# Two wide maxima of a unit move between the value products, and the turns get two buffers

## The chip, the cores and the metric

The kernel runs on one core of a Trainium2 chip. The core has TensorE (PE, with its weight loads listed apart as PEld), VectorE (DVE), ScalarE (ACT), GpSimd (POOL) and SyncE (SP), which here issues the DMAs. The metric is the device time of one launch, in microseconds (us). Before the change the median of three runs is 1690.89 us, from 1688.29 to 1691.36.

## The reference

Two layers of a diffusion backbone, each with an adaptive norm, a projection, attention, a SiLU gate and an output projection. Layer 0, which the change touches, is grouped-query attention: 16 heads share 4 key/value heads, a head has 64 columns. The 1024 latent tokens read 256 context keys and 1024 latent keys; the 256 context tokens read the context alone. All is in float32.

```python
def gqa_attend(q, k, v):
    s = jnp.einsum('bqhgd,bkhd->bhgqk', q, k).astype(jnp.float32) * (GQA_HEAD_DIM ** -0.5)
    p = jax.nn.softmax(s, axis=-1).astype(v.dtype)
    return jnp.einsum('bhgqk,bkhd->bqhgd', p, v)

def gqa_mixer(h, hc, p, cos, sin, with_ctx_out):
    ...
    k_all = jnp.concatenate([kc, k], axis=1)
    v_all = jnp.concatenate([vc, v], axis=1)
    o = sweep_query_blocks(lambda qb: gqa_attend(qb, k_all, v_all), q).reshape(B, S, GQA_WIDTH)
    y = (o * jax.nn.silu(g)) @ p["w_out"]
    ...
        oc = gqa_attend(qc, kc, vc).reshape(B, L, GQA_WIDTH)
```

## The kernel before

Layer 0's attention is worked off in 20 *units*: 16 *latent* units, one for each head (1024 queries, ten key tiles of 128, in `kts`), and four *context* units, one for each key/value head (its four heads' 256 queries, two key tiles). In order they are four latent, one context, four latent, one context, eight latent, two context. `Attention.run` takes them one after the other, with the order of PE, DVE and ACT as the code writes it; POOL and SP are ordered by a scheduler.

A latent unit has three stretches on PE:

- **Scores.** For each key tile a score tile `st` (128 keys by 1024 queries) is made of four pairs of products (L545): three for the split of queries and keys into a high and a low part, and one that subtracts each query's maximum, held in a row of `shift`. A pair is two products for the two halves of the queries, on rows 0 to 63 and 64 to 127 of the array, so 64 rows by 128 columns each. ACT makes the exponential `p` (L552). There are two buffers for `st`; the unit's value sum `avt` takes the place of one of them.
- **Turn and totals.** The maxima of a later unit, one for each query, stand in `m` with the queries on the partitions. `turn` (in `do_shift`) transposes them on PE into `mx` (L459), copies them on DVE to the row buffer `crow` (L461), and SP sends them from there to `shift` (L464). `crow` has one buffer. Then the totals of the softmax of an earlier unit are summed on PE, in `mx` (L645), and DVE transposes and inverts them there (L649, L650). `mx` has two buffers.
- **Value products.** `do_av` adds up 20 products with the values, two for each key tile (L600), each half in 64 columns of the array, so 128 rows by 64 columns. The trace has two records for each such product.

The maxima are made ahead. `next_maxima` hands out the steps of the units to come: a latent unit has ten *wide maxima*, eight over its latent keys (L421: two products of 512 columns into one `mx`, reduced by DVE in L430) and two over the context keys (L426, L432). One stands in front of each score tile of a latent unit (`count += 1` in `run`, then `scores_by_halves`). So during a latent unit the last six maxima of the next one and the first four of the one behind it are made, as a rule. The last latent unit (`last_lat`) has none left to make, and it is cut in two groups, of six and four tiles.

DVE also adds up the last four exponentials of a unit in pairs (L572, `pair_sum`), and POOL adds these sums and the first six exponentials (L586).

`run_turns` is called once for each group, between the scores and the value products, and runs all turns that are pending. Where a context unit's maxima have been finished together with those of a latent unit, it runs two, and three ahead of the last latent unit.

The same class makes layer 1's attention, with `WIDE` false: there the maxima are not wide, and `crow` comes from the common pool.

Of the kernel before, what the change touches and what calls it, by code (L numbers as in the profile page):

```python
# [11 lines left out]
F32R = mybir.dt.float32r  # L12
# [7 lines left out]
P = 128  # L20
# [9 lines left out]
WIDE = (True, False)  # L30


def raw(ap):
    return ap.bitcast(F32)
# [3 lines left out]
def hybrid_kernel(ctx: ExitStack, tc: tile.TileContext, ins: dict, out: bass.AP):  # L38
# [197 lines left out]
    class Plan:  # L236
# [8 lines left out]
        def run(self):  # L245
            engines = mybir.EngineType
            with tc.manual_schedule(engines={engines.PE, engines.Activation, engines.DVE, engines.Pool, engines.SP}):
                for _, _, fn, args in sorted(self.todo, key=lambda e: e[:2]):
                    fn(*args)
# [60 lines left out]
    class Attention:  # L310
# [134 lines left out]
        def do_shift(self, u):  # L445

            s = self.state[id(u)]
            if u["kind"] == "lat":
                m = self.sm.tile([P, 8], F32, name="m1", tag="m1")
                dve.reduce_max(m, s["m"], axis=AX.X)  # L450
            else:
                m = s["m"][:, :, 0]

            def turn():
                if not WIDE[self.l]:
                    t = self.ps_m.tile([P, 512], F32, name="mx", tag="mx")[:8, :P]
                else:
                    t = self.ps_m.tile([P, 1024], F32, name="mx", tag="mx")[:8, :P]
                pe.transpose(t, m, ident)  # L459
                r = self.sm.tile([8, P], F32R, name="crow", tag="crow", bufs=1)  # L460
                dve.tensor_copy(r, t)  # L461
                if HALVES[self.l]:
                    for n in range(2):
                        sp.dma_start(raw(s["crow"][n]), raw(r[4 * n:4 * n + 4, :]))  # L464
                else:
                    sp.dma_start(raw(s["crow"]), raw(r))

            self.turns.append(turn)

        def start_unit(self):  # L470
            u = self.units[self.started]
# [115 lines left out]
                s["sum"] = t  # L587
            s["total"] = ([s["sum"]] if held else []) + last

        def do_av(self, u, group, ps):  # L590

            s = self.state[id(u)]
            kts = u["kts"]
            if group[0] == kts[0]:
                if not WIDE[self.l]:
                    s["av"] = self.ps_o.tile([P, 512], F32, name="av", tag="av")
                s["v"] = self.load_v(u)
            for kt, p in zip(group, ps):
                for n in range(2):
                    pe.matmul(s["av"][64 * n:64 * n + 64, :], lhsT=s["v"][:, kt, u["vc"]:u["vc"] + 64],  # L600
                              rhs=p[:, n * 512:(n + 1) * 512], start=kt == kts[0], stop=kt == kts[-1])
            if group[-1] == kts[-1]:
                self.finish(u)
# [66 lines left out]

            self.totals.append(total)

        def run_turns(self):
            while self.turns:
                self.turns.pop(0)()

        def run(self, lead, ahead, extra, tail):

            count = lead
            parts = None  # L680
            with tc.manual_schedule(engines={mybir.EngineType.PE, mybir.EngineType.DVE, mybir.EngineType.Activation}):
                for t, u in enumerate(self.units):
                    kts = u["kts"]
                    for v in self.units[t:t + 2]:
                        self.load_v(v)
                    while self.started < min(t + 1 + ahead, len(self.units)):
                        self.start_unit()
                    whole = len(kts) > 4
                    cut = 6 if u is self.last_lat else 0

                    def one_more():
                        nonlocal count
                        count += 1
                        self.maxima(count, t + 1 + ahead)

                    for group in (kts[:cut], kts[cut:]):
                        if not group:
                            continue
                        end = group[-1] == kts[-1]
                        final = t == len(self.units) - 1 and end  # L700
                        p2s = [self.pp.tile([P, 2, 1024], F32, name="p", tag="p", bufs=5) for _ in range(len(group) // 2)]
                        ps = [p2[:, a, :] for p2 in p2s for a in range(2)]

                        late = not whole and t >= len(self.units) - 2
                        n1 = len(ps) - (4 if whole and end else 2 if late else 0)
                        for i, kt in enumerate(group):
                            self.run_deferred(self.step)
                            if HALVES[self.l]:
                                count += 1 if WIDE[self.l] else 2
                                self.scores_by_halves(u, kt, ps[i], self.next_maxima(count, t + 1 + ahead))  # L710
                            else:
                                self.do_scores(u, kt, ps[i], one_more)
                            self.step += 1
                            if i < n1:
                                self.add_up(u, [ps[i]], [])
                        if end and t + 2 < self.started:
                            self.state[id(self.units[t + 2])].pop("rest", lambda: None)()
                        if final:
                            tail()
                        if WIDE[self.l] and group[0] == kts[0]:  # L720
                            self.av_tile(u)
                        self.run_turns()
                        if late or final:
                            self.add_up(u, [], ps[n1:])
                        elif n1 < len(ps):
                            sums = [self.pair_sum(p2) for p2 in p2s[n1 // 2:]]
                            self.add_up(u, *(([], sums) if cut else (sums, [])))
                        if final:
                            self.run_deferred(self.step + 2)
                        gap = 0  # L730
                        while self.totals and (whole or late or final):
                            self.totals.pop(0)(gap)
                            gap += 3
                        if t % 2 and end:
                            if parts:
                                parts()
                            parts = extra.pop(0)() if extra else None
                        self.do_av(u, group, ps)
                        self.step += (2 + len(group)) // 3
                gap = 0  # L740
                while self.totals:
                    self.totals.pop(0)(gap)
                    gap += 3
            self.run_deferred(self.step)
# [373 lines left out]
    parts = [[ModPart(0, sec, q, 256, lambda: mp[0], 4, wk, ps_mod, ps_tp) for q in range(4)] for sec in range(2)]  # L1118
# [145 lines left out]
    def l0_open(at, st):  # L1264
        pool_ = st.enter_context(tc.tile_pool(name="shift0", bufs=1, **right))
        at.minus = pool_.tile([P, 4, P], F32R, name="minus")
        at.shift = pool_.tile([P, 512], F32R, name="shift")
        pool.memset(raw(at.shift), 0.0)
        for i in range(4):
            a, b = (ident[:, j:j + 1].broadcast_to([P, P]) for j in (i, 64 + i))  # L1270
            dve.scalar_tensor_tensor(at.minus[:, i, :], a, -1.0, b, op0=ALU.mult, op1=ALU.subtract)
# [89 lines left out]
    for g, pos in ((0, 4), (1, 9), (3, 18), (2, 19)):  # L1361
        units.insert(pos, ctxu[g])

    at = Attention(0, units, dict(scale=0.125, load=l0_load, scores=l0_scores, maxima=l0_maxima, mparts=1, open=l0_open, gaps=(4, 8, 11), kbufs=2, qbufs=3, vw=256))
    stE = ExitStack()
    with tc.tile_pool(name="wkg0a", bufs=4, **right) as wkg:
# [286 lines left out]
    for p_ in range(8):  # L1653
        for par in range(2):
            h = 2 * p_ + par
            units.append(dict(kind="lat", h=h, pair=p_, par=par, vg=(h // 4, 128 * (h // 2 % 2)), vc=64 * par,
                              kts=list(range(TT))))
    at = Attention(1, units, dict(scale=float(96 ** -0.5), load=l1_load, scores=l1_scores, maxima=l1_maxima, mparts=2, open=l1_open, gaps=(4, 6, 9),
                                  kbufs=3, qbufs=3, vw=128))
# [201 lines left out]
```

## Time and profile before

| | us |
|---|---|
| median of three runs | 1690.89 |
| the profiled execution, its own time | 1690.33 |
| its span, from the first to the last instruction | 1688.5 |
| first turn to last total of layer 0's attention | 376.7 to 741.9 |

The span is the part of the profiled execution that the trace shows; the 1.8 us around it belong to its own time too. A line of the page's groups reads: source line, engine, operation, output and inputs by the program's names, shape, count, then busy time and mean duration (ns) of one, then the idle time of the engine ahead of them and who ended it. The timeline lists instructions by their start and merges equal neighbours: with "x2", the two products of a pair. The idle time ahead and its releaser stand in brackets. PEclk, in the views by stretch, is the share of TensorE's full clock that was granted: three numbers from the end of a row, ahead of the DMA share and the GB/s.

```profile
L421 PE MATMUL mx<-KA,QA x256: 383/391/503, 317.2 to 685.0; 64*128 64x512 f32 x128
L600 PE MATMUL avt<-p,v x672: 592/592/1115, 376.9 to 740.4; 128*64 128x512 f32 x168
L461 DVE CAST crow<-mx x36: 267/278/280, 344.2 to 1562.5; 8x128 fp32r<-8x128 f32 x36
```

These three rows are of the views of single lines (shortest, median and longest duration in ns, first and last start in us): the wide maxima, the value products and the turns' copies.

### The profile page before, as it was taken

The numbers are of one execution on the slowest core, as the hardware profiler recorded it, in microseconds if no ns is written. First come the engines' busy times: TensorE is split into PE (matmuls) and PEld (weight loads), VectorE is DVE, ScalarE is ACT, GpSimd is POOL, SyncE is SP. The second block draws the span as 40 slices with busy tenths as digits, with TensorE's granted clock in tenths as the row PEclk, the third lists the DMA queues.
The fourth block names the chain that finished last, engine by engine and source line by source line (L and its number), as shares of the span: only waits on it lengthen the run. The fifth ranks groups of instructions, "written<-read, shape, count | busy, mean of one in ns | idle before, by whom it ended". The sixth has DMA issues, their size and how long they took to land. (4 is left out here: it accounts for less than half of the span.)

```text
span 1688.5 us, 27283 instructions
## 1 busy us (share of the span) xinstructions
PE 1646.4 (98%) x10236; PEld 1192.4 (71%) x10236; DVE 1044.3 (62%) x1652; ACT 642.1 (38%) x944; POOL 952.3 (56%) x632
## 2 busy tenths in 40 slices
PE   8999999999999999899989999999999999999998
PEld 5776768875555555468878798886766767667587
DVE  3765553457787887436675657754777777777231
ACT  4642212235444555423244533330434435334310
POOL 2673431128898998742344655450668778777521
PEclk9999999999999999999999999999999999999999
DMA  9547855532342522156434866766465555653351
GB/s 312 175 141 241 269 154 182 160 94 57 102 114 75 138 74 66 51 146 185 140 96 125 233 186 184 224 204 155 125 145 139 131 130 119 135 134 83 121 171 71
DMA packets 221116, 244.21 MB, mean 145 GB/s; under 512 B 23160, under 2 KB 160616, under 8 KB 220984
## 3 DMA queue, kind: packets, MB, share of 16 engines
q1 hardware_dynamic: 220560, 242.36, 51.4%
q8 instruction: 81, 1.33, 0.3%
q14 instruction: 51, 0.42, 0.1%
q10 hardware_dynamic: 424, 0.11, 0.0%
HBM read 168.62 MB, written 73.63 MB: 143 GB/s over the span
## 5 line engine op out<-in xcount | busy, mean ns | idle before, releaser
L552 ACT ACTIVATE p<-st 128x1024 f32<-128x1024 f32 x328 | 336.2, 1027 | 153.1 <-PE st L545 140.5
L586 POOL TENSOR_TENSOR acp<-acp,p 128x1024 f32<-128x1024 f32 x128 | 305.5, 2387 | 7.8
L394 DVE TENSOR_REDUCE m<-mx 128x1 f32<-128x512 f32 x256 | 176.1, 691 | 92.9 <-PE mx L392 87.7
L430 DVE TENSOR_REDUCE m<-mx 128x1 f32<-128x1024 f32 x128 | 150.4, 1220 | 68.3 <-PE mx L421 67.7
L586 POOL TENSOR_TENSOR acp<-p 128x1024 f32<-128x1024 f32 x34 | 81.5, 2399 | 184.7 <-ACT p L552 184.5
L586 POOL TENSOR_TENSOR acp<-acp,acd 128x1024 f32<-128x1024 f32 x60 | 142.4, 2374 | 20.1 <-DVE acd L572 16.9
L600 PE MATMUL avt<-p,v 128*64 128x512 f32 x672 | 151.0, 601 | 1.6 <-DVE crow L461 1.5
L572 DVE TENSOR_REDUCE acd<-p 128x512 f32<-128x1024 f32 x124 | 144.6, 1219 | 7.8 <-ACT p L552 7.8
L600 PE MATMUL av<-p,v 128*64 128x512 f32 x640 | 141.1, 595 | 0.0
L137 POOL TENSOR_TENSOR wb<-wraw,wa 128x512 fp32r<-128x512 f32 (+3 forms) x65 | 86.5, 1346 | 80.2 <-ACT wa L158 80.2
L94 PE MATMUL mm<-wa,hh 128*128 128x512 f32 (+2 forms) x336 | 127.3, 379 | 1.7 <-ACT hh L944 1.7
L545 PE MATMUL st<-QH,KH 64*128 64x512 f32 x320 | 122.8, 407 | 0.1
L96 PE MATMUL mm<-wa,hl 128*128 128x512 f32 (+2 forms) x336 | 121.4, 361 | 1.3 <-DVE hl L947 1.3
L95 PE MATMUL mm<-wb,hh 128*128 128x512 f32 (+2 forms) x336 | 121.2, 361 | 0.0
L545 PE MATMUL st<-QH,KL 64*128 64x512 f32 x320 | 118.1, 391 | 0.0
L545 PE MATMUL st<-QL,KH 64*128 64x512 f32 x320 | 117.6, 390 | 0.0
L600 PEld LDWEIGHTS avt<-p,v 128*64 128x64 f32 x672 | 46.6, 138 | 96.3 <-issue 85.2
L94 PE MATMUL y<-wa,oh 128*128 128x512 f32 (+1 forms) x296 | 114.0, 385 | 0.0
L96 PE MATMUL y<-wa,ol 128*128 128x512 f32 (+1 forms) x296 | 113.5, 384 | 0.0
L95 PE MATMUL y<-wb,oh 128*128 128x512 f32 (+1 forms) x296 | 113.5, 383 | 0.0
L600 PEld LDWEIGHTS av<-p,v 128*64 128x64 f32 x640 | 44.5, 137 | 88.3 <-issue 87.6
L94 PE MATMUL mm<-hh,wa 128*128 128x512 f32 (+1 forms) x264 | 103.2, 391 | 0.2 <-DVE qt L1734 0.2
(244 smaller groups left out, 4031.9 us busy)
## 6 DMA issues: line engine op xcount, KB each, us to landing
mraw<-in_l_w_mod SPq DMA_DIRECT2D x64, 256.0 KB
wraw<-in_l_w_in SPq DMA_DIRECT2D x28, 512.0 KB
KH<-k1h SPq DMA_DIRECT2D x32, 320.0 KB
KL<-k1l SPq DMA_DIRECT2D x32, 320.0 KB
rb<-rrow SPq DMA_DIRECT2D x72, 128.0 KB
mraw<-in_l_w_mod SPq DMA_DIRECT2D x16, 512.0 KB
QA<-q0h SPq DMA_DIRECT2D x32, 256.0 KB
wraw<-in_l_w_out SPq DMA_DIRECT2D x16, 512.0 KB
```

What stands on the lines that cost most here:

```text
L94: pe.matmul(ps, lhsT=lh(k), rhs=rh(k), start=first and i == 0, stop=False)
L95: pe.matmul(ps, lhsT=lh(k), rhs=rl(k), start=False, stop=False)
L96: pe.matmul(ps, lhsT=ll(k), rhs=rh(k), start=False, stop=last and i == len(ks) - 1)
L137: eng.tensor_sub(lo, a, b)
L394: dve.reduce_max(s["m"][:, i, n:n + 1], held["m"], axis=AX.X)
L430: dve.reduce_max(s["m"][:, i, 0:1], m, axis=AX.X)
L545: pe.matmul(ps[:, n * 512:(n + 1) * 512], lhsT=lh, rhs=rh, start=j == 0, stop=j == last)
L552: act.activation(p, ps, AF.Exp, scale=self.ops["scale"])
L572: dve.reduce_sum(t[:, ns], p2.rearrange("p a n -> p n a")[:, ns, :], axis=AX.X)
L586: pool.tensor_add(t, a, b)
L600: pe.matmul(s["av"][64 * n:64 * n + 64, :], lhsT=s["v"][:, kt, u["vc"]:u["vc"] + 64], rhs=p[:, n * 512:(n + 1) * 512], start=kt == kts[0], ...
```

## The change

Three things change, in layer 0 alone.

1. In a latent unit no maximum stands in front of the last two score tiles (`held_back`). The two stand in `do_av` instead, ahead of the value products of the sixth and of the eighth key tile.
2. `crow` comes from two tiles, allocated beside `shift`; the unit's number decides which.
3. `run_turns` runs only the turns of units up to the next latent one; those of context units that come later are left for a later call.

```diff
-                r = self.sm.tile([8, P], F32R, name="crow", tag="crow", bufs=1)
+                r = self.rows[self.units.index(u) % 2] if WIDE[self.l] else self.sm.tile([8, P], F32R, name="crow", tag="crow", bufs=1)
...
-            self.turns.append(turn)
+            self.turns.append((self.units.index(u), turn))
...
-        def do_av(self, u, group, ps):
+        def do_av(self, u, group, ps, between):
...
             for kt, p in zip(group, ps):
+                between.get(kt, lambda: None)()
...
-        def run_turns(self):
-            while self.turns:
-                self.turns.pop(0)()
+        def run_turns(self, upto=None):
+            while self.turns and (upto is None or self.turns[0][0] <= upto):
+                self.turns.pop(0)[1]()
...
+                    held_back = kts[-2:] if whole and WIDE[self.l] else []
+                    next_turn = t + 1
+                    while next_turn + 1 < len(self.units) and len(self.units[next_turn]["kts"]) <= 4:
+                        next_turn += 1
+                    if not WIDE[self.l]:
+                        next_turn = None
+
+                    def values_maximum():
+                        nonlocal count
+                        count += 1
+                        for _, parts in self.next_maxima(count, t + 1 + ahead):
+                            self.side_by_side(parts)
...
-                                count += 1 if WIDE[self.l] else 2
+                                if WIDE[self.l]:
+                                    count += 1 if kt not in held_back else 0
+                                else:
+                                    count += 2
...
-                        self.run_turns()
+                        self.run_turns(next_turn)
...
-                        self.do_av(u, group, ps)
+                        self.do_av(u, group, ps, {kts[5]: values_maximum, kts[7]: values_maximum} if held_back else {})
...
+        at.rows = [pool_.tile([8, P], F32R, name=f"crow{i}") for i in range(2)]
```

What this does to PE's order at the end of an ordinary latent unit, first before the change (`st` the last two score tiles, with a maximum `mx<-KA,QA` ahead of each, then turn, totals and value products):

```order
L421 MATMUL mx<-KA,QA 128x512 x2
L545 MATMUL st<-QA,KA 128x512 x2
L545 MATMUL st<-QA,KB 128x512 x2
L545 MATMUL st<-QL,KA 128x512 x2
L545 MATMUL st<-shift,minus 128x512 x2
L459 MATMUL mx<-ident,m_6377 8x128
L645 MATMUL mx<-acp,twos 32x256 x4
L600 MATMUL avt<-p,v 64x512 x20
L421 MATMUL mx<-KA,QA 128x512 x2
```

And the same place in the changed kernel:

```order
L545 MATMUL st<-shift,minus 128x512 x2
L459 MATMUL mx<-ident,m_6364 8x128
L646 MATMUL mx<-acp,twos 32x256 x4
L601 MATMUL avt<-p,v 64x512 x10
L421 MATMUL mx<-KA,QA 128x512 x2
L601 MATMUL avt<-p,v 64x512 x4
L421 MATMUL mx<-KA,QA 128x512 x2
L601 MATMUL avt<-p,v 64x512 x6
L421 MATMUL mx<-KA,QA 128x512 x2
```

Two pairs of L421 have left the scores and cut the 20 value products into ten, four and six; the last L421 opens the next unit in both.

DVE's order ahead of the last latent unit, before the change (L432 the reductions of context maxima, L461 the turns' copies, L572 the pair sums, L649 and L650 the totals):

```order
L432 TENSOR_REDUCE m<-mx 128x4 x4
L461 CAST crow<-mx 8x128 x3
L572 TENSOR_REDUCE acd<-p 128x512 x4
L649 STREAM_TRANSPOSE mx<-mx 128x256
L650 RECIPROCAL cr<-mx 128x8
```

And in the changed kernel, where the rows go on to the first totals inside the last latent unit:

```order
L432 TENSOR_REDUCE m<-mx 128x4 x2
L461 CAST crow_2950<-mx 8x128
L572 TENSOR_REDUCE acd<-p 128x512 x4
L650 STREAM_TRANSPOSE mx<-mx 128x256
L651 RECIPROCAL cr<-mx 128x8
L432 TENSOR_REDUCE m<-mx 128x4 x2
L461 CAST crow_2949<-mx 8x128
L461 CAST crow_2950<-mx 8x128
L650 STREAM_TRANSPOSE mx<-mx 128x256
L651 RECIPROCAL cr<-mx 128x8
```

Of the three copies in a row one is left; the other two come one group later, with a buffer each, and two reductions now stand behind the totals.

## The prediction

> **What bounds the kernel now.** I read the page first, then one unit of layer 0's attention as three stretches.
>
> ```profile
> span 1688.5 us, 27283 instructions
> PE 1646.4 (98%) x10236; PEld 1192.4 (71%) x10236; DVE 1044.3 (62%) x1652; ACT 642.1 (38%) x944; POOL 952.3 (56%) x632
> PE st L545 11%; PE av L600 8%; PE mx L392 4%; PE mm L94 2%; PE mm L95 2%; PE mm L96 2%; PE y L94 2%; PE y L96 2%; PE y L95 2%; PE mx L402 1%; PE mx L645 1%; DVE wb L137 0%; DVE tl L88 0%; POOL q_rs L120 0%; POOL t L1736 0%
> ...
> 593.78:605.80 12.02, 12.02 (x106) 9.15 (x104) 11.38 (x11) 9.80 (x10) 11.73 (x6) 1.00 0.18 47
> 605.80:606.94 1.14, 0.85 (x12) 0.27 (x10) 1.14 (x3) 1.06 (x2) 1.06 (x2) 1.00 0.36 50
> 606.94:615.67 8.73, 8.73 (x44) 2.78 (x40) 4.64 (x6) 0.00 (x0) 8.50 (x4) 1.00 0.35 98
> ```
>
> TensorE is busy for 98% of the span, and the chain that ended last runs on it. The three rows below the dots are a unit's scores, its turn with the totals, and its value products (length, then busy time of PE, weight loads, DVE, ACT, POOL). TensorE fills the first and the third stretch; in the third DVE works 4.64 of 8.73 us. So whatever adds TensorE time in the value products adds to the end, whatever DVE has free there, and a maximum is worth taking out of the scores only if TensorE itself is what sets their pace. There are 16 latent units, 15 of which carry ten maxima each.
>
> **What a maximum costs among the scores.** Two tiles with maxima before each, against two tiles without any (the last latent unit has none):
>
> ```profile
> 601.22 0.45 PE L545 MATMUL st<-QA,KA 64*128 64x512 f32 x2
> 603.60 0.43 PE L545 MATMUL st<-QA,KA 64*128 64x512 f32 x2
> 604.56 0.39 PE L421 MATMUL mx<-KA,QA 64*128 64x512 f32 x2
> 604.79 0.40 PE L545 MATMUL st<-QA,KA 64*128 64x512 f32 x2
> ...
> 712.39 0.49 PE L545 MATMUL st<-QA,KA 64*128 64x512 f32 x2 [0.29 <-ACT p L552]
> 714.76 0.50 PE L545 MATMUL st<-QA,KA 64*128 64x512 f32 x2 [0.26 <-ACT p L552]
> ...
> 603.53 0.18 PEld L545 LDWEIGHTS st<-QA,KA 64*128 64x128 f32 x2 [0.21 <-ACT p L552]
> ```
>
> From tile 6 (601.22) to tile 8 (603.60) it takes 2.38 us with maxima; without them 714.76 - 712.39 = 2.37 us. The score buffer is one of two, and tile 8 may start only when the exponential of tile 6 has read it: the weight load at 603.53 is released by ACT. A maximum takes its own 604.79 - 604.56 = 0.23 us, but it fills a wait that is there anyway. Without the one before tile 8, TensorE stands at that same wait. Tile 9 may start when the exponential of tile 7 has ended, which by the same reckoning on the 15 units is 0.05 us earlier than it starts now, not 0.46. So I take **0.05 us x 15 = 0.7 us gained**, with bounds of 0 and 30 x 0.23 = 6.9 us.
>
> **What it costs among the value products.** The two kinds of product use differently shaped parts of the array (64 rows by 128 columns, and 128 by 64), and the rows show what a change from one to the other takes:
>
> ```profile
> 615.14 0.60 PE L600 MATMUL avt<-p,v 128*64 128x512 f32 x2
> 615.67 0.50 PE L421 MATMUL mx<-KA,QA 64*128 64x512 f32 x2
> ...
> 605.48 0.39 PE L545 MATMUL st<-shift,minus 64*128 64x512 f32 x2
> 605.80 0.27 PE L459 MATMUL mx<-ident,m 128*8 128x128 f32 x1
> ...
> 453.76 0.39 PE L545 MATMUL st<-shift,minus 64*128 64x512 f32 x2
> 454.22 0.65 PE L600 MATMUL avt<-p,v 128*64 128x512 f32 x2
> ...
> 606.94 0.20 PEld L600 LDWEIGHTS avt<-p,v 128*64 128x64 f32 x4 [0.41 <-ACT p L552]
> 607.42 0.14 PEld L600 LDWEIGHTS avt<-p,v 128*64 128x64 f32 x2 [0.29 <-issue]
> 607.85 0.14 PEld L600 LDWEIGHTS avt<-p,v 128*64 128x64 f32 x2 [0.29 <-issue]
> ```
>
> A pair of value products follows the one before after 607.85 - 607.42 = 0.43 us. From the last pair to a maximum it is 615.67 - 615.14 = 0.53. From a maximum back to a value product is not in this trace; the bounds are 605.80 - 605.48 = 0.32 (from scores to the turn's other shape) and 454.22 - 453.76 = 0.46 (from scores to value products, where the exponential has to be waited for too). I take 0.36, nearer to the first because of that wait. The first pair after such a change takes 607.42 - 606.94 = 0.48. An inserted maximum thus costs 0.53 + 0.36 + 0.48 - 2 x 0.43 = 0.51 us, **30 x 0.51 = 15.3 us**; with the bounds 0.47 and 0.61 it is 14.1 to 18.3. The lower end of all is 0.23, if the changes of shape were hidden: 6.9 us.
>
> [...]
>
> Behind each inserted product stands its reduction on DVE:
>
> ```profile
> 606.34 4.66 DVE L572 TENSOR_REDUCE acd<-p 128x512 f32<-128x1024 f32 x4
> 611.41 0.21 DVE L650 RECIPROCAL cr<-mx 128x8 f32<-128x8 f32 x1
> 567.19 0.21 DVE L650 RECIPROCAL cr<-mx 128x8 f32<-128x8 f32 x1
> ```
>
> DVE has the pair sums and the total's reciprocal first, until 611.62. The first inserted maximum comes five tiles in, at about 606.6 + 5 x 0.87 = 611, and has the buffer that the turn's copy freed long before; the second comes at about 613.2 and needs the total's buffer, free 1.6 us earlier. Neither waits. In the two units with two totals the first inserted maximum needs the first total's buffer, free at 567.40 in one of them, by about when it comes: at most 0.2 us each, **0.4 us**.
>
> **What the turns give.** With no maximum in front of the last two tiles, the turn and the totals need not wait for the last reduction:
>
> ```profile
> 606.37 0.64 PE L645 MATMUL mx<-acp,twos 128*32 128x256 f32 x8 [0.29 <-DVE m L430]
> 601.61 4.61 DVE L430 TENSOR_REDUCE m<-mx 128x1 f32<-128x1024 f32 x4
> ...
> 376.66 0.27 PE L459 MATMUL mx<-ident,m 128*8 128x128 f32 x1
> 376.86 0.65 PE L600 MATMUL avt<-p,v 128*64 128x512 f32 x2
> ...
> 419.54 0.27 PE L459 MATMUL mx<-ident,m 128*8 128x128 f32 x1
> 420.28 0.64 PE L645 MATMUL mx<-acp,twos 128*32 128x256 f32 x8
> ...
> 441.62 0.27 PE L459 MATMUL mx<-ident,m 128*8 128x128 f32 x1
> 442.28 0.64 PE L645 MATMUL mx<-acp,twos 128*32 128x256 f32 x8 [0.39 <-DVE m L430]
> ```
>
> From the turn (605.80) to the totals (606.37) it takes 0.57 us, because the second buffer is read by the reductions until 606.22. Where nothing has to be waited for, the turn is left after 376.86 - 376.66 = 0.20. Nine units like this gain 0.36 each, 3.2 us. The double turns (419.54 and another) become single ones, 0.74 to 0.20, 1.1 us. The single ones behind them (441.62 and another, 0.66) become double ones, whose totals wait for the first copy: I estimate 0.7, so 0.1 us is lost.
>
> The triple turn ahead of the last latent unit is a case by itself:
>
> ```profile
> 671.47:681.34 9.87, 9.57 (x51) 3.05 (x49) 5.79 (x8) 1.07 (x2) 9.29 (x4) 1.00 0.36 102
> 693.39:696.90 3.51, 0.73 (x6) 0.28 (x5) 0.88 (x3) 1.04 (x2) 3.43 (x2) 0.91 0.01 1
> 696.90:699.45 2.55, 1.08 (x8) 0.20 (x8) 0.33 (x2) 0.00 (x0) 0.63 (x1) 0.50 0.01 2
> 699.45:709.99 10.54, 10.54 (x41) 3.21 (x42) 5.09 (x6) 0.00 (x0) 4.72 (x2) 0.83 0.13 27
> ...
> 696.47 0.28 DVE L461 CAST crow<-mx 8x128 fp32r<-8x128 f32 x1 [2.48 <-DMA shift<-crow]
> 699.12 0.28 DVE L461 CAST crow<-mx 8x128 fp32r<-8x128 f32 x1 [2.37 <-DMA shift<-crow]
> ```
>
> Turn, totals and value products take 9.87 us in the unit before (671.47) and 3.51 + 2.55 + 10.54 = 16.60 here. Two copies wait 2.48 and 2.37 us for a DMA to empty the one row buffer, TensorE stands still behind them, and the granted clock then falls to 0.50 and averages 0.83 over the value products. With one turn here, and the other two behind the last latent unit's first six tiles, from two buffers, I expect 0.20 + 0.57 + 8.73 = 9.5: **7.1 us gained**. The two moved turns cost 0.7 us there, by the estimate above. Their DMAs now stand on SP behind the layer's next loads; the rows are needed some 10 us later. POOL, busy for 11.73 + 1.06 + 8.50 = 21.3 of a unit's 21.9 us, gets the same work; in four places its first addition goes behind two gate products of an earlier unit, and its sums are needed a unit later. A longer unit gives it room. [...]
>
> **Sum.** 15.3 + 0.4 + 0.7 + 0.1 lost, 0.7 + 3.2 + 1.1 + 7.1 gained: 16.5 - 12.1 = +4.4 us. The profiled execution took 1690.33 us itself (0.56 below the median of the runs, 1690.89), so I predict **1694.7 us**, 0.2% above the median; with the bounds of the shape change it is 1693.5 to 1697.7. A measurement of this kernel can tell about 0.2%, 3.4 us, from no change, so this stands on the edge.
>
> **Rivals.**
> - *The changes of shape are hidden* (the other side). An inserted maximum costs its own 0.23 us, since the weights are loaded beside the running value product. It decides at (12.1 - 1.2) / 30 = 0.36 us for one maximum, where 30 of them and the lesser losses equal the gains. Time: 6.9 + 1.2 - 12.1 = -4.0, 1686.3 us. Against it stand 0.53 and 0.48 beside 0.43. [...] Chance 0.12.
> - *The scores shrink by what is taken out.* Tiles 8 and 9 come 0.46 us earlier; 6.9 instead of 0.7 us gained: 1688.5 us. Against it: 2.37 us without maxima, 2.38 with. Chance 0.15.
> - *DVE becomes late in the value products.* The inserted reductions queue behind the pair sums; if those run over 1.6 us late, the second maximum stands and the value products behind it. At 0.3 us in each of 15 units: +4.5, 1699.2 us. For it: 11.38 us of DVE in 12.02 us of scores; against it, DVE is idle from 611.62. Chance 0.12.
> - *The turns still wait*, so that the change doesn't do what it says: +6.5, 1701 us. Against it: two turns in a row now use different buffers. Chance 0.06.
>
> **How the numbers follow.** The forecast has 0.55: 0.33 slower by over 0.2% and 0.22 within it. Hidden changes: 0.10 faster, 0.02 same. Shrinking scores: 0.14 same, 0.01 faster. The last two: 0.18 slower. That makes 0.11 faster, 0.38 same, 0.51 slower. The range runs from 1687.5 (below the shrinking scores, leaving out most of the hidden changes) to 1699.0 (about the late DVE, without the waiting turns).
>
> **What would show it.** In the profile of the changed kernel: a value product 0.53 us before each inserted maximum and another about 0.36 us after it; value products of 9.7 instead of 8.73 us; scores of still about 12.0 us; 0.20 us from turn to totals; no copy that waits for a DMA, and a clock of 1.00 from 690 to 715 us. The forecast is wrong if the value products grow by 0.5 us only, or the scores fall to 11.5.

## The result, and the profile after

The changed kernel takes **1699.66 us** (median of six runs, 1697.91 to 1701.62), the one before 1691.12 beside it (six runs, 1688.29 to 1696.41). The ratio is 1.0047, with a 95% interval of 1.0030 to 1.0065: slower by half a per cent. The forecast was 1694.7, its range ended at 1699.0.

The page's head, then six stretches by the view of stretches (length, busy time of PE, weight loads, DVE, ACT and POOL, clock, DMA): the scores, the turn with the totals, and the value products of an ordinary unit, then the turn and the value products ahead of the last latent unit, and last the whole attention of layer 0, from 0.8 us before the first maximum ahead of a score tile to the end of the last total.

```profile
span 1697.8 us, 27283 instructions
PE 1660.6 (98%) x10236; PEld 1190.1 (70%) x10236; DVE 1049.0 (62%) x1652; ACT 641.7 (38%) x944; POOL 953.6 (56%) x632
...
602.63:614.59 11.96, 11.93 (x103) 8.77 (x101) 9.57 (x9) 9.74 (x10) 11.65 (x7) 1.00 0.18 45
614.59:615.36 0.77, 0.77 (x12) 0.24 (x10) 0.46 (x2) 0.75 (x2) 0.77 (x1) 1.00 0.00 0
615.36:625.26 9.90, 9.90 (x48) 2.98 (x45) 7.40 (x8) 0.36 (x1) 9.55 (x5) 1.00 0.39 108
705.19:705.96 0.77, 0.77 (x11) 0.24 (x9) 0.46 (x2) 0.71 (x2) 0.77 (x1) 1.00 0.00 0
705.96:715.87 9.91, 9.91 (x52) 3.22 (x48) 7.41 (x8) 0.37 (x1) 7.83 (x4) 1.00 0.13 28
363.07:748.60 385.53, 382.45 (x2619) 201.54 (x2617) 284.16 (x297) 189.50 (x199) 317.63 (x151) 1.00 0.33 89
```

The same attention in the kernel before:

```profile
364.02:741.92 377.90, 368.81 (x2620) 205.91 (x2618) 277.48 (x296) 189.57 (x199) 317.52 (x152) 0.99 0.34 91
```

Attention is 7.63 us longer. Cut into its stretches, the scores give +0.12, turns and totals -8.59, the value products +16.09. TensorE's idle time in it fell from 9.09 to 3.08 us (length less busy time), and its busy time rose by 13.64: the change removed waits, and paid more than that in TensorE's time. The ordinary unit shows it: scores 11.96 against 12.02, turn and totals 0.77 against 1.14, value products 9.90 against 8.73. The clock of the triple turn's place is 1.00 now.

The other 1.7 us of the profiled run (1699.64 against 1690.33) lie outside attention. In the kernels below, which leave the rest of the program alone, span less attention lies between 1307.3 and 1315.0 us (before 1310.6, after 1312.3), so I read nothing from it, and no run shows where it comes from; I compare attention.

PE's timeline of the ordinary unit, from its turn to the next unit's first products:

```profile
614.59 0.27 PE L459 MATMUL mx<-ident,m 128*8 128x128 f32 x1
614.79 0.64 PE L646 MATMUL mx<-acp,twos 128*32 128x256 f32 x8
615.36 4.51 PE L601 MATMUL avt<-p,v 128*64 128x512 f32 x20
619.80 0.50 PE L421 MATMUL mx<-KA,QA 64*128 64x512 f32 x2
620.23 1.94 PE L601 MATMUL avt<-p,v 128*64 128x512 f32 x8
622.10 0.50 PE L421 MATMUL mx<-KA,QA 64*128 64x512 f32 x2
622.53 2.80 PE L601 MATMUL avt<-p,v 128*64 128x512 f32 x12
625.26 0.49 PE L421 MATMUL mx<-KA,QA 64*128 64x512 f32 x2
```

From the turn to the totals 0.20 us, as forecast. From a maximum back to the value products 620.23 - 619.80 = 0.43, and 0.43 again at 622.10: I had taken 0.36. No row has an idle time: as far as the trace shows, TensorE waits for no other engine here. DVE in the same place:

```profile
615.10 4.66 DVE L572 TENSOR_REDUCE acd<-p 128x512 f32<-128x1024 f32 x4
619.70 0.44 DVE L650 STREAM_TRANSPOSE mx<-mx 128x256 f32<-128x256 f32 x1
620.17 0.21 DVE L651 RECIPROCAL cr<-mx 128x8 f32<-128x8 f32 x1
620.35 1.23 DVE L430 TENSOR_REDUCE m<-mx 128x1 f32<-128x1024 f32 x1
622.65 1.23 DVE L430 TENSOR_REDUCE m<-mx 128x1 f32<-128x1024 f32 x1 [1.07 <-PE mx L421]
```

DVE waits for the second maximum, not TensorE for DVE.

### The profile page after: what moved, and what is told of

It reads as the page before. It is cut to its first block, busy times and chain, and to the rows that moved or that the text cites. A ratio compares the mean times of both kernels' runs of the same rounds, so it can differ in the third digit from the quotient of the medians.

```text
span 1697.8 us, 27283 instructions
## 1 busy us (share of the span) xinstructions
PE 1660.6 (98%) x10236; PEld 1190.1 (70%) x10236; DVE 1049.0 (62%) x1652; ACT 641.7 (38%) x944; POOL 953.6 (56%) x632
## 5 line engine op out<-in xcount | busy, mean ns | idle before, releaser
L601 PE MATMUL avt<-p,v 128*64 128x512 f32 x672 | 155.9, 601 | 0.1
L586 POOL TENSOR_TENSOR acp<-acp,acd 128x1024 f32<-128x1024 f32 x60 | 142.2, 2371 | 14.1 <-DVE acd L572 10.8
L572 DVE TENSOR_REDUCE acd<-p 128x512 f32<-128x1024 f32 x124 | 144.7, 1220 | 7.8 <-POOL rb L665 7.8
L137 POOL TENSOR_TENSOR wb<-wraw,wa 128x512 fp32r<-128x512 f32 (+3 forms) x65 | 87.7, 1362 | 80.7 <-ACT wa L158 80.7
L392 PE MATMUL mx<-KH,QH 64*128 64x512 f32 x256 | 102.3, 405 | 0.3 <-DVE m L403 0.3
```

The source lines that it names most:

```text
L137: eng.tensor_sub(lo, a, b)
L392: pe.matmul(held["m"][:, cs], lhsT=q[:, t * P:(t + 1) * P], rhs=k[:, ks], start=j == 0, stop=j == len(pairs) - 1)
L572: dve.reduce_sum(t[:, ns], p2.rearrange("p a n -> p n a")[:, ns, :], axis=AX.X)
L586: pool.tensor_add(t, a, b)
```

## The experiments

Each kernel is the changed one with the edit shown. Attention is measured as above, with the same 0.8 us ahead of the first maximum in every kernel, so that differences do not contain it; "before" is 377.90 us. Each of these figures is from one traced execution.

### The turns alone, and the maxima alone

All ten maxima back in front of the score tiles, with the turns' part of the change kept:

```diff
-                    held_back = kts[-2:] if whole and WIDE[self.l] else []
+                    held_back = []
```

> Only the turns are changed (two row buffers, turns no further than the next latent unit); all ten maxima stay among the scores. Theory (the loss is the price of the maxima between the value products, the turns are a gain of their own): value products 8.73 us a unit, scores 12.0, the triple turn's 16.60 us becomes 9.9, the two moved turns cost 0.7 us; layer 0's attention, from the first maximum ahead of a score tile to the first output product, falls from 377.9 to about 371.8 us and the time to about 1685. Rival (part of the loss lies outside the attention, in DMAs or the clock, and comes with the turns too): the attention falls as above, but the time stays at 1688 or above.

And the reverse, the two maxima between the value products with one row buffer and every pending turn run at each call:

```diff
-                r = self.rows[self.units.index(u) % 2] if WIDE[self.l] else self.sm.tile([8, P], F32R, name="crow", tag="crow", bufs=1)
+                r = self.sm.tile([8, P], F32R, name="crow", tag="crow", bufs=1)
...
-                    if not WIDE[self.l]:
-                        next_turn = None
+                    next_turn = None
...
-        at.rows = [pool_.tile([8, P], F32R, name=f"crow{i}") for i in range(2)]
```

> Only the maxima are changed (two of ten between the value products); the turns have one row buffer and all pending ones run at once, as before. Theory: value products 9.90 us a unit, 0.36 us less from turn to totals in the ordinary units, the triple turn still waits for its DMAs; the attention grows from 377.9 to about 392 us, the time to about 1705. Rival (outside the attention): attention 392, time about 1708.

The turns alone: 1686.88 us (ten runs) against 1691.65, ratio 0.9971 (0.9961 to 0.9981), 0.3% **faster**. Attention is 373.58, 4.3 us shorter. The expectation had 371.8; 1.25 of the 1.8 us between them are in the scores of one unit (12.00 to 13.25 us), the subject of the last section. The maxima alone: one run of 1697.51, attention 388.41, 10.5 us longer. The two parts of the change pull in opposite directions, and the one that is slower is the larger.

The maxima alone missed the expectation by 3.6 us, and that taught something: the stall of the triple turn vanishes there too (6.06 to 1.30 us), since the last context unit's maxima are now finished only in the value products, and their turns come later by themselves. So about 6 us of gain, with the clock (1.00 in the mean of this attention, 0.99 before), are in both halves and count once. In the three units with double turns the one row buffer now hurts (value products of 10.98, 10.91 and, ahead of the last latent unit, 10.51 us instead of 9.90). The first of them, in DVE's timeline and then PE's:

```profile
422.51 0.28 DVE L461 CAST crow<-mx 8x128 fp32r<-8x128 f32 x1 [2.93 <-DMA shift<-crow]
...
428.12 0.50 PE L421 MATMUL mx<-KA,QA 64*128 64x512 f32 x2 [1.01 <-DVE cr L651]
```

The second copy waits 2.93 us for the DMA, the totals' reciprocal behind it is late, and the second inserted maximum stands for its buffer. The two buffers prevent that, so they are needed by the maxima, too.

### One maximum, or two side by side

Only the last tile without a maximum, and one maximum ahead of the eighth tile's value products; then both maxima of the change together at that one place:

```diff
-                    held_back = kts[-2:] if whole and WIDE[self.l] else []
+                    held_back = kts[-1:] if whole and WIDE[self.l] else []
...
-                        self.do_av(u, group, ps, {kts[5]: values_maximum, kts[7]: values_maximum} if held_back else {})
+                        self.do_av(u, group, ps, {kts[7]: values_maximum} if held_back else {})
```

> As the changed kernel, but only the last score tile is without a maximum, and one maximum stands between the value products (ahead of the eighth tile). Theory (each costs 0.58 us by the change of shape on both its sides): value products 9.32 us a unit, turn to totals still 0.20; the attention is about 376.5 us. Rival (the second of the two pays, by waiting for a buffer behind DVE's pair sums): this one stands where the second stood, so value products of 9.3 would be met by both, but the step into it would be longer than 0.53 us.

```diff
-                        self.do_av(u, group, ps, {kts[5]: values_maximum, kts[7]: values_maximum} if held_back else {})
+                        self.do_av(u, group, ps, {kts[7]: lambda: (values_maximum(), values_maximum())} if held_back else {})
```

> As the changed kernel, but both maxima stand together ahead of the eighth tile's value products. Theory (shape): one change into and out of the shape is paid instead of two, 0.53 + 0.23 + 0.43 + 0.48 - 0.86 = 0.81 us a unit instead of 1.17: value products 9.55 us, attention about 380 us. Rival (the price is by the maximum, whatever stands beside it): value products 9.90 us.

One maximum adds 0.58 us to a unit's value products (8.73 to 9.31), half of the change's 1.17; attention 377.11, one run of 1689.39. The pair adds 0.81 (9.55) instead of 1.17; attention 379.25, one run of 1690.99. PE's timeline of the pair:

```profile
616.05 0.73 PE L421 MATMUL mx<-KA,QA 64*128 64x512 f32 x4
616.71 2.79 PE L601 MATMUL avt<-p,v 128*64 128x512 f32 x12
```

Two maxima and the way back take 616.71 - 616.05 = 0.66 us; one took 0.43. So the second adds its own 0.23 and no more: two maxima apart pay for the change of shape twice, a pair once.

### The shape itself

The same two places, with the maxima made by products of the value products' shape (128 rows, 64 columns, four products for each maximum in place of two). The two halves of the rows hold the same numbers here, so the product is twice the score, and the maximum is halved after the reduction; the first of the two kernels takes plain float32 for it. Then with 128 rows and 128 columns, a third shape:

```diff
+                    for c in (0, 64):
+                        pe.matmul(m[c:c + 64, ns], lhsT=raw(q[:, i * P + c:i * P + c + 64]), rhs=raw(k[:, ns]), start=True, stop=True)
+                dve.reduce_max(s["m"][:, i, 0:1], m, axis=AX.X)
+                dve.tensor_scalar(s["m"][:, i, 0:1], s["m"][:, i, 0:1], 0.5, None, op0=ALU.mult)
```

> As the changed kernel, but the two maxima between the value products are made in the shape of the value products (128 rows by 64 columns, plain float32, both copies of the head added and the maximum halved by one more small DVE operation). Each takes four steps of 0.43 us instead of one of 0.23. Theory (shape): the steps into and out of it are 0.43 like all others and the first value product after it too, so value products of 8.73 + 2 x 4 x 0.43 = 12.2 us. Rival (any foreign product costs a step, by its waits on semaphores or its weights): 0.53, 0.43 and 0.48 stay, about 12.5 us.

```diff
+                    pe.matmul(m[:, ns], lhsT=q[:, i * P:(i + 1) * P], rhs=k[:, ns], start=True, stop=True)
```

> As the changed kernel, but the two maxima between the value products use all 128 rows and 128 columns of the array (two products one after the other, both copies of the head added and the maximum halved by one more small DVE operation). Each takes two steps of 0.23 us. If any change of shape costs: 0.23 us more for each than in the changed kernel, value products about 10.35 us. If only the split of the rows costs: no longer step on either side, 8.73 + 2 x 0.46 = 9.65 us.

PE's timeline of the first, then of the second (their lines L420 and L419 are the maxima, L628 and L626 the value products):

```profile
617.53 1.89 PE L420 MATMUL mx<-KA,QA 128*64 128x512 f32 x8
619.25 1.89 PE L628 MATMUL avt<-p,v 128*64 128x512 f32 x8
```

```profile
599.68 0.60 PE L626 MATMUL avt<-p,v 128*64 128x512 f32 x2
600.21 0.73 PE L419 MATMUL mx<-KA,QA 128*128 128x512 f32 x2
600.88 1.94 PE L626 MATMUL avt<-p,v 128*64 128x512 f32 x8
```

In the same shape nothing is paid at either edge: four products (two records each) in 619.25 - 617.53 = 1.72 us, 0.43 each, as in the value products themselves. A unit's value products take 12.17 us, against 12.2 by the theory and 12.5 by the rival. The whole is slower (1730.92 us, one run), since a maximum takes 1.72 us there; that was expected. In the third shape the edges cost again: 600.21 - 599.68 = 0.53 on the way in, and 600.88 - 600.21 = 0.67 for two single steps and the way back, like the pair above; value products of 10.36 us, against 10.35 and 9.65 (1701.46 us, one run). So the cost is not one of 64 rows or of the maxima.

One rival is left by these two kernels: the type changes with the shape. The value products are plain float32, and so are the maxima of the first kernel; the maxima and scores elsewhere are float32r, the program's other type of 32-bit numbers. The trace of before tells the two apart. First the start of attention, where the shape changes and both sides are float32r; then a place in the projections, where the shape stays and the type changes to plain float32 and back (`tp`, transposes):

```profile
364.50 0.28 PE L95 MATMUL mm<-hlc,wa 128*128 128x256 f32 x1
364.62 0.28 PE L96 MATMUL mm<-hhc,wb 128*128 128x256 f32 x1
364.82 0.50 PE L421 MATMUL mx<-KA,QA 64*128 64x512 f32 x2
365.16 0.40 PE L545 MATMUL st<-QA,KA 64*128 64x512 f32 x2
365.40 0.39 PE L545 MATMUL st<-QA,KB 64*128 64x512 f32 x2
```

```profile
84.74 0.40 PE L95 MATMUL mm<-wb,hh 128*128 128x512 f32 x1
84.97 0.39 PE L96 MATMUL mm<-wa,hl 128*128 128x512 f32 x1
85.20 0.60 PE L927 MATMUL tp<-ident,xt 128*128 128x128 f32 x4
85.56 0.48 PE L94 MATMUL mm<-wa,hh 128*128 128x512 f32 x1
85.87 0.40 PE L95 MATMUL mm<-wb,hh 128*128 128x512 f32 x1
```

Where only the shape changes, the step is 364.82 - 364.62 = 0.20 instead of 0.12, and the first product of the new shape takes 0.34 instead of 0.24. Where only the type changes, the step to the transposes is 85.20 - 84.97 = 0.23, as between the products ahead of them, and the four transposes with the product behind them take 85.87 - 85.20 = 0.67 (4 x 0.11 + 0.23; 0.11 is also the step between the four at 24.80, 0.60 us in all as here). The cost is one of **a change of shape**, in all the changes seen here.

### The last maximum at the seam

The last tile's maximum behind the last value product, ahead of the next unit's first one, where the shape changes anyway:

```diff
+            between.get("end", lambda: None)()
             if group[-1] == kts[-1]:
                 self.finish(u)
...
-                        self.do_av(u, group, ps, {kts[5]: values_maximum, kts[7]: values_maximum} if held_back else {})
+                        self.do_av(u, group, ps, {"end": values_maximum} if held_back else {})
```

(`held_back` has the last tile alone.)

> As the changed kernel, but only the last score tile is without a maximum, and that one stands behind the last value product, ahead of the next unit's first maximum, which has the same shape. Theory (shape): it costs its own 0.23 us and no change; turn to totals 0.20; the attention falls from 377.9 to about 370 us and the time to about 1683, 1 to 2 us below the kernel with the turns alone. Rival (two maxima in a row wait for DVE and the two buffers): 0.5 us or more a unit are lost at the next unit's second maximum, and it is no faster than the turns alone.

1689.10 us (ten runs), ratio 0.9988 (0.9978 to 0.9997), and no faster than the turns alone, as the rival said. The value products fall back to 8.73, but the scores behind a moved maximum grow by 0.52 to 0.58 (0.25 in the last latent unit): the maximum's own 0.23, and about 0.34, less than the rival's 0.5, at the next unit's second maximum, which waits for a buffer that DVE still reads:

```profile
621.63 0.40 PE L545 MATMUL st<-shift,minus 64*128 64x512 f32 x2
622.20 0.50 PE L421 MATMUL mx<-KA,QA 64*128 64x512 f32 x2 [0.17 <-DVE m L430]
```

The step is 622.20 - 621.63 = 0.57 instead of 0.23. Attention 376.68, 3.1 us longer than with the turns alone.

### Which half of the turns' part

The limit on the turns with one row buffer, and two row buffers without the limit, both with all maxima in front of the score tiles:

> Of the turns' change only the limit on which turns run (turns only up to the next latent unit); one row buffer as before, all ten maxima ahead of the score tiles. Two turns then stand in a row inside the last latent unit with one row buffer. Theory: TensorE was stopped by the third turn, whose copy held a buffer of the maxima and totals; with two turns the second copy's wait for the DMA (about 2.4 us) lies behind value products, so the limit alone gives what the whole turn change gave: turn and totals ahead of the last latent unit 6.06 to about 1.1 us, value products 10.5 to 8.7, attention about 4.3 us shorter than before. Rival: each wait for the one row buffer stops TensorE; 2.4 us of it come back inside the last latent unit, and attention is 2 us shorter only.

> Of the turns' change only the two row buffers; all pending turns run at each call as before, all ten maxima ahead of the score tiles. Three turns then stand in a row ahead of the last latent unit, with two row buffers. Theory: the first two copies need not wait, so both buffers of the maxima and totals come free at once; only the third copy waits for a DMA (about 2.1 us), with value products on TensorE. Turn and totals there fall from 6.06 to about 1.6 us, the clock does not fall, value products 10.5 to 8.7; attention 5 to 6 us shorter than before. Rival: the third copy's wait stops TensorE for 2 us or more, turn and totals 3.7 us or more, and attention is 3 us shorter or less.

My theory failed in both, and the limit alone did worse than even its rival: it gains nothing (1690.08 us, one run; attention 378.06), the two buffers alone gain 3.4 us (1684.96, one run; 374.55), nearer to their rival. PE's timeline with the limit alone, and two stretches of it; then PE's with the buffers alone:

```profile
714.92 6.80 PE L601 MATMUL avt<-p,v 128*64 128x512 f32 x24 [4.45 <-DVE crow L461]
...
711.00:712.00 1.00, 0.00 (x0) 0.00 (x0) 0.00 (x0) 0.00 (x0) 0.92 (x2) 1.00 1.11 334
715.00:716.00 1.00, 1.00 (x4) 0.38 (x6) 0.44 (x2) 0.00 (x0) 1.00 (x1) 0.50 0.00 0
```

```profile
695.42 4.94 PE L601 MATMUL avt<-p,v 128*64 128x512 f32 x22 [1.58 <-DVE crow L461]
```

My theory had the waiting copy beside running value products. But once no maxima are left to make, the value sum itself takes one of the two buffers `mx` (`av_tile`), here the one that the last copy holds. With the limit alone the two turns only move into the last latent unit and wait there: 4.45 us, and the clock falls to 0.50 behind it. With the buffers alone the third of three turns waits, and TensorE for 1.58 us; 3.4 of the 4.3 us that both give together are there already. Only both together leave no copy waiting for a DMA: in the changed kernel the 36 copies have idle time ahead of them for PE alone.

### A total ahead of the turns

With the turns alone, an ordinary unit's totals still wait 0.28 us for the last reduction, the very wait that the change removes by moving the maxima. It goes as well if the two change places, since the buffer that is free first then goes to the longer of the two, and the turn finds the other one free. First wherever a total is pending, then only where exactly one turn and one total are:

```diff
+                        due = sum(next_turn is None or i <= next_turn for i, _ in self.turns)
+                        if WIDE[self.l] and len(self.totals) == 1 and due == 1 and (whole or late or final):
+                            self.totals.pop(0)(gap)
+                            gap = 3
                         self.run_turns(next_turn)
```

> The turns of the change (two row buffers, turns only up to the next latent unit), all ten maxima back ahead of the score tiles, and in addition one total of an earlier unit stands ahead of the turns instead of behind them. With the turns alone, the totals wait 0.28 us for the last reduction in the usual unit, and turn and totals take 1.12 us there. Theory: the buffer that the totals take now is free earlier, and their 0.57 us cover the wait of the turn. Turn and totals fall to about 0.8 us in the nine or ten usual units, 3 us in all; attention 7 to 7.5 us shorter than before (4.3 with the turns alone), time about 1684. Rival: DVE must now wait for the totals before it copies the turn and adds in pairs, so its work ends 0.6 us later, and the units with two totals or two turns wait for DVE's transposes; the gain goes there, and the time stays at about 1687.

> As the run with one total ahead of the turns (e7_swap), but the total stands ahead only where exactly one turn and one total are pending; where there are two turns or two totals, the order is that of the turns alone. In e7_swap turn and totals took 0.77 instead of 1.13 us in the usual units, but 1.76 and 2.13 instead of 1.40 and about 1.57 (two turns, two totals), and 1.76 instead of 1.31 in the last latent unit, since the second turn waits for the total's reciprocal. Theory: these five places go back to their values with the turns alone, 2.3 us, and the usual units keep their 0.36: attention about 8 us shorter than before (5.7 in e7_swap, 4.3 with the turns alone), time about 1682.5. Rival: what a unit gains ahead of the value products is given back at the next score tiles, where TensorE waits for ACT or DVE; then attention stays about 6 us shorter and the time at 1685.

The first: 1685.12 us (five runs), ratio 0.9964 (0.9951 to 0.9978), attention 372.20, 5.7 us shorter than before and not the 7 to 7.5 expected: the places with two turns or two totals lost, as the rival said, though not the whole gain. The second: **1682.24 us** (six runs), ratio 0.9947 (0.9934 to 0.9961), attention 371.02. It has the lowest median and the shortest attention of all, though the intervals of the two overlap. Turn and totals take 0.77 us in the ordinary units without a maximum moved; in the second kernel's timeline of PE, without a wait:

```profile
605.36 0.64 PE L646 MATMUL mx<-acp,twos 128*32 128x256 f32 x8
605.93 0.27 PE L459 MATMUL mx<-ident,m 128*8 128x128 f32 x1
606.13 0.65 PE L601 MATMUL avt<-p,v 128*64 128x512 f32 x2
```

Its attention was to be 8.0 us shorter than before and is 6.9: the five places gave back 2.0 of the 2.3 us, and the scores are 0.8 us longer than in the first of the two runs, nearly all of it at one maximum in PE's timeline:

```profile
551.53 0.50 PE L421 MATMUL mx<-KA,QA 64*128 64x512 f32 x2 [1.29 <-DVE m L430]
```

This wait is the subject of the last section. One further place does not gain: ahead of the last latent unit the value sum, which has a buffer `mx` there, waits for the total's reciprocal (0.72 us), and turn and totals take 1.56 us instead of 1.14 with the turns alone.

## Why the prediction was right and wrong

Direction and mechanism were right, a size was wrong: the sum was +4.4 us, attention alone measured +7.6, and the medians differ by 8.5.

**The step that failed** is "From a maximum back to a value product is not in this trace ... I take 0.36, nearer to the first because of that wait". It is 0.43, and the term "30 x 0.51 = 15.3 us" becomes 30 x 0.58 = 17.5, from 1.17 us in each ordinary unit. The true value lay inside the bounds of 14.1 to 18.3 given with it, near the upper one. The runs show what it is made of. On the way in, the step to the maximum is 0.53 instead of 0.43 (+0.10). The first product of the new shape itself is longer by 0.10: with maxima of the third shape, 0.33 from the first product to the second. The step back adds 0.10 over the product's own 0.23 (0.33 from the second product to the value products; both in the trace with the third shape, where the two products of a maximum start one after the other), and the first value product takes 0.48 (+0.05). That is 0.35 for the edges, once per group, and 0.23 for each product in it: 0.58 for one, 0.81 for two side by side, as measured. I had charged the longer first step to the value product behind the maximum, but not to the maximum itself. The trace of before showed it: of the maximum behind the last value product, at 615.67 (quoted in the prediction), the next rows of PE's timeline are

```profile
616.01 0.40 PE L545 MATMUL st<-QA,KA 64*128 64x512 f32 x2
616.25 0.39 PE L545 MATMUL st<-QA,KB 64*128 64x512 f32 x2
```

From that maximum to the next product of its own shape it is 616.01 - 615.67 = 0.34 us, and from there on 0.24. The same 0.33 stands behind a product that starts after a wait without any change of shape: the one at 712.39, quoted in the prediction, is followed at 712.72. Either of my two bounds was a step out of a product that came 0.22 to 0.23 us after one of its own shape (605.25 to 605.48, 453.54 to 453.76); a lone maximum between two changes has none of its shape ahead of it.

The other steps:

- *Scores, 0.7 us gained.* About 0.05 us in an ordinary unit, as forecast; but one unit gave 0.70 back (last section), so the scores came out 0.1 longer. Together with the maxima that is 3.0 of the 3.2 us between the forecast of +4.4 and the measured +7.6 of attention.
- *The two units with two totals, 0.4 us.* Their value products grew by 1.36 and 1.35 instead of 1.17: 0.19 each.
- *Turns and totals.* Double turns 0.54 and 0.55, the moved turns +0.74: right. Of the nine units at 0.36 us each, seven gained that; the two with two totals waited less before and gained 0.27, 0.2 us less in all.
- *The triple turn, 7.1 us.* Turn, totals and value products take 0.77 + 9.91 us there, of which two maxima are 1.17, so 9.51: right. The halves of this part tell what each edit does. The two buffers alone bring 16.60 us down to 3.43 + 8.73. The limit alone brings it to 1.13 + 8.73, and loses as much inside the last latent unit (5.83 + 6.73 instead of 0.57 + 5.30). That the low clock would go with the long wait was my estimate, in the 8.73 us of the sum; where the wait is gone, the clock is 1.00 (705.96 to 715.87).
- *Rivals.* The changes of shape are not hidden (0.58 us for a maximum, not its own 0.23), the scores do not shrink (11.96 against 12.02 us in the ordinary unit), no copy waits for a DMA, and DVE is not late in the ordinary unit's value products (it waits 1.07 us for the second maximum).
- *The range.* 1690.33 + 7.63 is 1698.0, inside it. What took the time past 1699.0 is the rest of the program, 1.7 us longer in the profiled run. What makes it longer stays open; in the kernels that leave it alone it took 3.3 us less to 4.4 us more than before. The ends of the range came from the sum alone; the runs' own spread (1688.29 to 1691.36 beforehand) had to be added, and I had not.

## What to carry to other kernels

A product that filled a wait cost next to nothing here: the scores gained 0.05 us a unit when two maxima left them. In a stretch that TensorE fills it cost more than its own time, between products of a different shape: 0.58 us for a lone one, 2.5 times its own 0.23. So group such products (0.81 for two) or leave them where the wait is. Before moving work to remove a wait for a buffer, look whether two users of that buffer can change places: that gave the same 0.36 us in the ordinary units without a product moved, though it lost 0.3 to 0.6 us in each place where two turns or two totals met. And ask of a second buffer how many users stand in a row: alone, with three of them, it gave 3.4 us; with an order that has at most two, 4.3; the order alone gave nothing.

## What was not expected of the hardware

**A subtraction on DVE ended 0.55 to 0.59 us after POOL's operation.** The 0.70 us in the scores come from one subtraction on DVE (w_out's split, L137) at the start of one unit. In the changed kernel, on POOL and on DVE, with the maximum that came late:

```profile
554.90 2.38 POOL L586 TENSOR_TENSOR acp<-p 128x1024 f32<-128x1024 f32 x1
...
555.88 1.95 DVE L137 TENSOR_TENSOR wb<-wraw,wa 128x512 fp32r<-128x512 f32 x1 [1.78 <-ACT wa L158]
...
559.02 0.51 PE L421 MATMUL mx<-KA,QA 64*128 64x512 f32 x2 [0.55 <-DVE m L430]
```

The subtraction ends at 557.83, 0.55 us after POOL's addition (557.28). The same instruction took 0.69 us in the kernel before and 2.67 in the fastest one, and in the eleven traces where I compared it, it ended 0.55 to 0.59 us after the POOL operation that was running when it began. It is not alone: of this line's 42 subtractions of this size on DVE in the trace of before, 28 began while POOL ran an operation on 128x512 elements or more. They ended 0.55 to 0.59 us after it and took 0.69 to 1.93 us. The other 14, ten begun with POOL idle and four with POOL in an operation on 128x4 or 128x8 elements, took 0.68 to 0.69. So for the 28 the length follows from when POOL's operation ends. The reductions behind the subtraction are late, and TensorE waits for a buffer. In the eleven traces this unit's scores took 11.96 to 12.02 us where the subtraction took up to 1.02 us, 12.71 to 12.76 at 1.95 or 1.96, and 13.02 to 13.48 at 2.27 to 2.67. POOL's addition here was longer where it began while the subtraction ran: 2.84 and 2.85 us in two of the eleven traces, 2.38 to 2.40 in the others. What makes one wait for the other is not shown: no run here moved the subtraction.

**The clock fell during a wait and stayed low behind it.** With the limit on the turns alone TensorE stood still for 4.45 us; the granted clock was 1.00 until about 714.4, 4.0 us into the wait, and then 0.50 for some 3.4 us, while TensorE worked again. In the kernel before, a wait of 2.58 us was enough: the clock fell 2.0 us into it, at about 696.3, and stayed at 0.50 for 6.8 us, until about 703.1, through a second wait of 1.47 us. After the 1.58 us of the run with two buffers alone the clock stayed at 1.00 (695.42 to 704.15). What sets these times is not shown.
